# A one-core hybrid decoder layer: the load order of the DeltaNet stage, the planner's turns of small products, and the engine that forms the decayed queries

## The chip, the core and the metric

The kernel runs on one core of a Trainium2 chip. That core has five engines with instruction queues of their own: TensorE (PE in the profile, with its weight loads as PEld), VectorE (DVE), ScalarE (ACT), GpSimd (POOL) and SyncE (SP), which here does nothing but issue DMAs. The metric is the device time of one execution in microseconds. The kernel before was timed in three runs: 966.21, 965.89 and 964.76 us, median 965.89 us.

## The reference, cut to what matters

One layer is computed: 528 tokens (16 meta tokens and 512 of the input) of width 2048, normalised, projected by one wide matrix into the inputs of three mixers, whose outputs are joined and projected back. The change touches the first mixer, gated DeltaNet, with 6 heads of 128. Per chunk of tokens it needs the inverse of a unit lower triangular matrix, built from key products and decays:

```
a_mat = where(strict, einsum('bhncd,bhnsd->bhncs', kb, kc) * decay, 0)
u, w  = triangular_solve(eye + a_mat, [v * beta, kb * exp(g)])
qk    = where(causal, einsum('bhncd,bhnsd->bhncs', qc, kc) * decay, 0)
q_dec = qc * exp(g)
k_dec = kc * exp(g_last - g)
# per chunk, in order:
v_new = u - w @ s
o     = q_dec @ s + qk @ v_new
s     = s * g_last + k_dec^T @ v_new
```

The other two mixers are gated linear attention (GLA, 5 heads) and forgetting attention (5 heads); then come the output projection, the residual and a last normalisation.

## The kernel before, in words

All matrices are fp32. The wide products split their operands into two parts and use three matmuls with 512 (or, in a seven-product scheme, 264) moving columns; these read a weight tile of 128x128 each. The small products inside the mixers use plain fp32.

The work is written as generators (chains). A planner, `Weave` (L210 to L355), runs them against a table of costs (`cost`, L201) and emits one fixed program: every engine's instructions stand in the planned order, and the chip cannot change it. When an operand comes later than planned, the engine waits at that instruction and everything behind it on that engine waits too. A DMA is planned as one shared queue: bytes at 350 KB per microsecond, and then a fixed time to land (`DMAL`, L85, for loads; `STL` for stores to DRAM).

The planner distinguishes two kinds of TensorE work. An operation is "light" (L184) when it has under 64 moving columns, or fewer than 128 rows or columns of weights. In the DeltaNet stage these are the tiles `pm` (32x32), `pn` (64x64) and `pym` (16 rows), in GLA the tile `pss`. All else counts as heavy, the 128x128 products of the DeltaNet core (`pks`, `p1`, `po`) too. Lines L340 to L351 set the turns:

```
ran = t - self.since
if self.mode:
    other = ran + (sum(o.dur for o in c[3]) if c[3][0].light else 0.0) > LIGHT
else:
    other = ran >= HEAVY
...
    like = [x for x in self.chains if isinstance(x[3], list) and x[3][0].eng == "P"
            and x[3][0].light == kind and x[4] <= t + NEAR]
```

A turn of light work ends when it would pass `LIGHT`, if heavy work is ready within `NEAR`; when the best candidate is itself heavy, only what has already run is compared with `LIGHT`, and one more light list may be taken. A heavy turn ends after `HEAVY` (1.5), if light work is ready within `NEAR`. All of these are the planner's microseconds.

The stages in order of time are these. Up to 491 us the wide input projections run (`pz`, `pg`, `pbdz`, `px`). While they run, the score matrices of both DeltaNet head groups (`ans[0]`, `ans[1]`, three heads each) are made in `an_block` and stored to DRAM, and `inverse` (L695) inverts their 32x32 diagonal blocks on VectorE in a tile `ab`, stored to `sc2` at its end. Sixteen further projection blocks, the FILL list (`pbgq`, `pbfq`, `pbgz`, `pbfz`), are independent of all this. From 476 us on the planner puts them between the small products, and later takes the output projection's matmuls (`po` with 512 columns) for the same purpose.

The DeltaNet stage begins in `phase_b` (L1020). For each group g of three heads:

- `dn_rows(g)` (L1054) issues loads on SP: the score matrices `an`, keys `kT`, scaled values `vp`, queries `qT` and decayed keys `kd`. Group 1 waits until group 0 is through.
- `dn_group(g)` (L1077) loads the inverted blocks: `xc` and `xm` from `sc2`, and the meta rows `kdm`, `vpm`. Group 1 waits for `e_first`, which group 0 sets when its loads are out and its `levels` chain is started.
- `levels` and `level64` (L1099, L1139) combine 32x32 inverses to 64 and 128 with `pm` and `pn`; `state0` (L1163) makes the state after the meta tokens with `pym`.
- `core` (L1200) walks four blocks of 128 tokens. `pre` (L1182) prepares each block: it loads the decays `eg`, masks them on GpSimd into `at`, takes exponentials on ScalarE, multiplies `eg` by the queries (the decayed queries) on GpSimd, and forms the masked scores. `tail` (L1235) makes the block's output and normalises it.

## Time and profile before

| | us |
|---|---|
| median of three runs | 965.89 (964.76 to 966.21) |
| the profiled execution's own time | 967.15 |
| its span, first to last instruction | 964.6 |
| busy in the span: PE | 949.2 |
| PEld | 847.6 |
| DVE | 750.6 |
| ACT | 559.6 |
| POOL | 49.6 |

All instructions carry line L280, where the planner emits them, so the profile is read by tile names. Names are cut at digits: `an` stands for the score tiles, and also for the `eg` and `at` of `core`, which live in the same memory; `p` is `p1`; `po` with 128 columns belongs to `tail` and with 512 columns to the output projection. A fp32 matmul shows as two records. `SPq` is the queue on which SP issues DMAs. `PEclk` is the granted TensorE clock, 1.00 at full speed.

### The profile page before, as it was taken

To read this page: it belongs to the slowest core of one execution; us is meant where nothing else is said; L and a number is where in the kernel's file an instruction comes from. 1 tells how busy PE (TensorE), PEld (TensorE's weight loads), DVE (VectorE), ACT (ScalarE), POOL (GpSimd) and SP (SyncE) were. 2 spreads that over 40 slices of the span, in tenths; PEclk is the share of its full clock that TensorE was granted. 3 is DMA by queue.
4 is the path that set the end of the run, shared out by engine and by line. 5 is a ranking of instruction groups with operands and counts; after the bars stand their busy time and mean duration, and the time that the engine had idled before them with its cause. 6 is when DMAs were issued, how large, how long until landed. Compare 5 with 4: busy or idle time off the path is not lost.

```text
span 964.6 us, 18891 instructions
## 1 busy us (share of the span) xinstructions
PE 949.2 (98%) x7301; PEld 847.6 (88%) x7301; DVE 750.6 (78%) x1338; ACT 559.6 (58%) x1192; POOL 49.6 (5%) x94
## 2 busy tenths in 40 slices
PE   9999999999999999999999999999999999999996
PEld 7888999999999999999987897778787887888885
DVE  7986888888988787888983565886867976889874
ACT  7865566667656575754423675647555664335534
POOL 0000000000000000000010221101010100000000
PEclk9999999999999999999999899999999999999999
DMA  9933234436552535543188335424244246733105
GB/s 340 364 128 132 89 122 160 156 105 180 148 169 90 157 118 170 156 147 97 56 300 278 119 78 197 139 87 143 83 140 155 79 141 212 279 99 121 44 23 174
DMA packets 78893, 144.09 MB, mean 149 GB/s; under 512 B 14781, under 2 KB 35005, under 8 KB 78804
## 3 DMA queue, kind: packets, MB, share of 16 engines
q1 hardware_dynamic: 78516, 142.63, 45.0%
q8 instruction: 57, 0.93, 0.4%
q10 hardware_dynamic: 288, 0.27, 0.1%
q14 instruction: 32, 0.26, 0.1%
HBM read 119.26 MB, written 23.61 MB: 148 GB/s over the span
## 4 chain that ended last, share of the span: by engine, by line
PE 91%; DVE 3%; DMA 3%; ACT 2%; issue 1%; POOL 0%; DVEq 0%; SPq 0%; ACTq 0%; POOLq 0%
PE px L280 38%; PE po L280 11%; PE pz L280 6%; PE ps L280 6%; PE pbgz L280 5%; PE pbfz L280 5%; PE pbfq L280 4%; PE pbdz L280 2%; PE pfa L280 2%; PE pks L280 1%; PE pg L280 1%; PE pfw L280 1%; PE pss L280 1%; PE pbgq L280 1%; PE pgo L280 1%; DMA sc<-ab 1%
## 5 line engine op out<-in xcount | busy, mean ns | idle before, releaser
L280 DVE SCALAR_TENSOR_TENSOR lp<-a,hp 128x1024 fp32r<-128x1024 f32 x90 | 110.4, 1227 | 37.4 <-ACT hp L280 35.1
L280 ACT CAST hp<-a 128x1024 fp32r<-128x1024 f32 x90 | 94.4, 1049 | 71.8 <-PE px L280 44.0
L280 PE MATMUL px<-xh,hp 128*128 128x264 f32 x432 | 123.9, 287 | 0.0
L280 PE MATMUL px<-xh,lp 128*128 128x264 f32 x432 | 122.7, 284 | 0.0
L280 PE MATMUL px<-xl,hp 128*128 128x264 f32 x432 | 122.7, 284 | 0.0
L280 PE MATMUL px<-tah,hp 128*128 128x264 f32 x288 | 84.0, 292 | 0.0
L280 PE MATMUL px<-tbh,lp 128*128 128x264 f32 x288 | 82.3, 286 | 0.0
L280 PE MATMUL px<-tbh,hp 128*128 128x264 f32 x288 | 82.1, 285 | 0.0
L280 PE MATMUL px<-tbl,hp 128*128 128x264 f32 x288 | 82.0, 285 | 0.0
L280 PE MATMUL px<-tah,lp 128*128 128x264 f32 x288 | 81.9, 284 | 0.0
L280 PE MATMUL px<-tal,hp 128*128 128x264 f32 x288 | 81.8, 284 | 0.0
L280 PEld LDWEIGHTS px<-xh,hp 128*128 128x128 f32 x432 | 81.4, 188 | 0.0
L280 PEld LDWEIGHTS px<-xl,hp 128*128 128x128 f32 x432 | 81.2, 188 | 0.0
L280 PEld LDWEIGHTS px<-xh,lp 128*128 128x128 f32 x432 | 81.2, 188 | 0.0
L280 PE MATMUL po<-ho,oh 128*128 128x512 f32 x136 | 54.6, 402 | 0.0
L280 PEld LDWEIGHTS px<-tbh,hp 128*128 128x128 f32 x288 | 54.3, 189 | 0.1
L280 PEld LDWEIGHTS px<-tah,hp 128*128 128x128 f32 x288 | 54.2, 188 | 0.1
L280 ACT CAST hp<-s 128x1024 fp32r<-128x1024 f32 x36 | 37.8, 1050 | 28.4 <-PE px L280 20.9
L280 PEld LDWEIGHTS px<-tal,hp 128*128 128x128 f32 x288 | 54.3, 188 | 0.0
L280 PEld LDWEIGHTS px<-tbl,hp 128*128 128x128 f32 x288 | 54.2, 188 | 0.0
L280 PEld LDWEIGHTS px<-tah,lp 128*128 128x128 f32 x288 | 54.2, 188 | 0.0
L280 PEld LDWEIGHTS px<-tbh,lp 128*128 128x128 f32 x288 | 54.2, 188 | 0.0
(416 smaller groups left out, 2614.5 us busy)
## 6 DMA issues: line engine op xcount, KB each, us to landing
a<-in_w_in SPq DMA_DIRECT2D x72, 512.0 KB, 3.9
o<-in_w_out SPq DMA_DIRECT2D x20, 512.0 KB, 3.2
rgz<-in_w_in SPq DMA_DIRECT2D x10, 512.0 KB, 5.8
rfq<-in_w_in SPq DMA_DIRECT2D x10, 512.0 KB, 4.4
rfz<-in_w_in SPq DMA_DIRECT2D x10, 512.0 KB
xs<-in_xT SPq DMA_DIRECT2D x16, 264.0 KB, 5.5
fraw<-in_w_first SPq DMA_DIRECT2D x16, 256.0 KB
xt<-in_xtok SPq DMA_DIRECT2D x8, 512.0 KB
```

What stands on the lines that cost most here:

```text
L280: self.pin(op.call(*op.a, **op.kw))
```

## The change

The first part merges the two `dn_rows` chains into one with a new order: both groups' `an` first, then group 0's `kT` and `vp`, then a wait for `e_first`, and behind it group 0's `qT` and `kd` and all the rest of group 1. The second changes two constants of the planner: `LIGHT` from 3.0 to 2.2 and `NEAR` from 0.05 to 0.4. The third forms the decayed queries by `VT`, a scalar_tensor_tensor on VectorE, in place of a tensor_tensor on GpSimd.

```diff
-LIGHT, SLACK, DMAL, STL = 3.0, 0.25, 1.1, 2.5
-HEAVY, NEAR = 1.5, 0.05
+LIGHT, SLACK, DMAL, STL = 2.2, 0.25, 1.1, 2.5
+HEAVY, NEAR = 1.5, 0.4
...
-        for g in range(2):
-            W.go(dn_rows(g), LP + 0.1 * g, f"dnr{g}")
+        W.go(dn_rows(), LP, "dnrows")
...
-    def dn_rows(g):
-        s = gs[g]
-        if g:
-            yield e_rows[0]
-        s.an = yield Get(big_s, f"an{g}", (P, NN, P))
-        for b in range(NB):
-            yield e_an[g, b]
-        yield SP.dma_start(out=s.an, in_=ans[g])
-        e_anl[g].set()
-        s.kT = yield Get(big_s, f"kT{g}")
-        s.qT = yield Get(big_s, f"qT{g}")
-        for j in range(H):
-            yield from fetched(("dk", H * g + j), s.kT[:, j], Ev())
-        s.vp = yield Get(big_s, f"vp{g}", (P, NN, P))
-        yield SP.dma_start(out=s.vp, in_=vps[g])
-        for j in range(H):
-            yield from fetched(("dq", H * g + j), s.qT[:, j], Ev(), False)
-        s.kd = yield Get(keep_s, f"kd{g}")
-        yield SP.dma_start(out=s.kd, in_=kds[g])
-        e_rows[g].set()
+    def dn_rows():
+        for g in range(2):
+            gs[g].an = yield Get(big_s, f"an{g}", (P, NN, P))
+            for b in range(NB):
+                yield e_an[g, b]
+            yield SP.dma_start(out=gs[g].an, in_=ans[g])
+            e_anl[g].set()
+        for g in range(2):
+            s = gs[g]
+            s.kT = yield Get(big_s, f"kT{g}")
+            s.qT = yield Get(big_s, f"qT{g}")
+            if g:
+                yield e_first
+            for j in range(H):
+                yield from fetched(("dk", H * g + j), s.kT[:, j], Ev())
+            s.vp = yield Get(big_s, f"vp{g}", (P, NN, P))
+            yield SP.dma_start(out=s.vp, in_=vps[g])
+            if not g:
+                yield e_first
+            for j in range(H):
+                yield from fetched(("dq", H * g + j), s.qT[:, j], Ev(), False)
+            s.kd = yield Get(keep_s, f"kd{g}")
+            yield SP.dma_start(out=s.kd, in_=kds[g])
+            e_rows[g].set()
...
-        yield G.tensor_tensor(out=eg, in0=eg, in1=s.qT[:, :, ts], op=ALU.mult)
+        yield VT(out=eg, in0=eg, in1=s.qT[:, :, ts], op=ALU.mult)
```

## The prediction

> **What bounds the kernel now.** The page first, to see which engine sets the time:

> ```profile
> span 964.6 us, 18891 instructions
> PE 949.2 (98%) x7301; PEld 847.6 (88%) x7301; DVE 750.6 (78%) x1338; ACT 559.6 (58%) x1192; POOL 49.6 (5%) x94
> ```

> TensorE is busy for 949.2 of 964.6 us, and the change takes no matmul away. So time can come only from two places: moments in which TensorE stands, and moments in which it runs slowly. Its waits by tile come next (tile, releaser, total us, times, longest):

> ```profile
> PE pkd L280 <- DVE gst L280: 1.2, 2, 0.8
> PE pm L280 <- DVE uc L280: 1.0, 1, 1.0
> PE pss L280 <- issue: 0.9, 1, 0.9
> PE po L280 <- ACT f L280: 0.9, 1, 0.9
> ```

> Each is small. Two of them, `pm` and `po`, lie in the DeltaNet stage. For slow running I read the busy times by windows of 3.41 us there: first of everything, with the granted clock after the engines, then of the instructions that touch tile `pbgz` alone, the wide filler.

> ```profile
> 523.31:526.73 3.42, 3.22 (x151) 2.89 (x144) 1.85 (x6) 2.35 (x5) 0.00 (x0) 1.00 0.77 253
> 526.73:530.14 3.41, 3.41 (x38) 2.70 (x37) 0.92 (x5) 2.45 (x7) 0.00 (x0) 1.00 1.02 386
> 530.14:533.55 3.41, 3.41 (x34) 2.17 (x35) 0.00 (x0) 0.80 (x2) 0.00 (x0) 0.50 0.99 366
> 533.55:536.97 3.42, 3.42 (x120) 3.19 (x110) 1.52 (x3) 2.47 (x5) 1.75 (x4) 1.00 0.08 22
> 536.97:540.38 3.41, 3.41 (x19) 2.66 (x18) 2.21 (x7) 2.77 (x4) 0.00 (x0) 0.50 0.02 5
> ```

> ```profile
> 523.31:526.73 3.42, 1.20 (x5) 1.03 (x6) 0.00 (x0) 1.00 0.77 253
> 526.73:530.14 3.41, 0.46 (x2) 0.02 (x1) 0.00 (x0) 1.00 1.02 386
> 533.55:536.97 3.42, 0.00 (x0) 0.00 (x0) 0.00 (x0) 1.00 0.08 22
> ```

> The clock is 0.50 in exactly two windows, 530.14 to 533.55 and 536.97 to 540.38. Each follows a window that held almost nothing but small products: 0.46 and 0.00 us of wide matmuls. The window with 1.20 us of them was followed by full speed. PE was busy through the bad windows too (3.41 of 3.41), so standing still isn't the cause here; the kind of work is. What the half clock costs is read from the chain of waits, in order of time (start, length, what):

> ```profile
> 506.40 7.79 DMA sc<-ab
> 514.25 5.31 DMA xc<-sc
> 525.60 1.59 PE pbgz L280 x6
> 530.41 2.86 PE pbgz L280 x6
> 534.34 1.54 PE pn L280 x24
> 536.74 1.34 PE pks L280 x6
> 538.08 1.28 PE pbgz L280 x3
> 539.36 2.02 PE pn L280 x24
> 541.38 0.86 PE pks L280 x6
> ```

> The same pieces at both speeds: six `pbgz` 2.86 against 1.59 (+1.27), six `pks` 1.34 against 0.86 (+0.48), three `pbgz` 1.28 against half of 1.59 (+0.48), 24 `pn` 2.02 against 1.54 (+0.48). Together **2.7 us**; 3.4 is the most that two half-speed windows can cost.

> **The change, part by part.**

> *Shorter turns (`LIGHT` 3.0 to 2.2).* By the cost table of the code a `pn` or `pym` list counts 0.68, the first `pm` list 0.67, the second 1.34. The turn before 530.14 was `pym`, two `pn`, `pym`: 2.8 with the entry of 0.1, under 3.0. Under 2.2 it is cut after three lists, and the two other long turns of the stage after two or three. The longest turn then counts 2.15 or so where it counted 3.5, and a heavy turn of 1.5 stands behind it, two lists of three wide matmuls, 1.59 us on the chip. A window of 3.41 us then holds at least about 1 us of wide work, near the 1.20 that kept full speed and far from 0.46. I take both half-speed windows as gone: **-2.7**, with ends 0 and -3.4. Wide work has to be at hand for it: the chain shows `pbgz` before and after each of the long turns. More turns cost entries, by the timeline:

> ```profile
> 705.83 0.51 DVE L280 SCALAR_TENSOR_TENSOR qx<-gqT,gd 128x256 f32<-128x256 f32 x1
> 706.08 0.39 PE L280 MATMUL pbgz<-xl,hbgz 128*128 128x512 f32 x1
> 706.31 0.40 PE L280 MATMUL pbgz<-xh,lbgz 128*128 128x512 f32 x1
> 706.64 0.43 PE L280 MATMUL pss<-qx,kx 64*32 64x32 f32 x33
> ```

> Wide to wide is 0.23 us, wide to small 0.33: 0.1 for an entry. Three more turns are **+0.3**. GLA hardly changes: its lists of 64 products count 1.79, and two of them passed 3.0 already.

> *`NEAR` 0.05 to 0.4.* The planner may now place a small product up to 0.4 us before its operand. If the chip were as late as the plan, each of some 18 turns (6 in DeltaNet; in GLA four lists of `gla_levels` for each of three pairs) could wait 0.4 more, 7 us in all. But at 706.64 above, the operand `qx` was done at 706.34, 0.30 ahead, and this is the shortest lead among the GLA turns: the chip is earlier than the plan there. So 0.1 here and there, I take **+0.2**, ends 0 and +7. The transposes with 16 columns in the projection stage become candidates only after ScalarE operations that follow their operand, so `NEAR` moves none of them.

> *The loads.* The DMA issues from 490.4 to 506.4, up to the store `sc<-ab`, and from there to 519.6, when `xc` is in:

> ```profile
> DMA packets 1896, 5.65 MB, mean 353 GB/s; under 512 B 205, under 2 KB 205, under 8 KB 1895
> qT<-spdq SPq DMA_DIRECT2D x3, 256.0 KB
> kd<-kds SPq DMA_DIRECT2D x1, 768.0 KB
> ```

> ```profile
> rfq<-in_w_in SPq DMA_DIRECT2D x2, 512.0 KB
> an<-ans SPq DMA_DIRECT2D x1, 768.0 KB
> kT<-spdk SPq DMA_DIRECT2D x2, 264.0 KB
> ```

> Ahead of the store, `qT` and `kd` (1536 KB) leave and group 1's `an` (768 KB) enters: 768 KB less, 2.2 us at 353 GB/s. Between store and `xc`, `an` and two `kT` leave (1296 KB), 3.7 us. I expect the 13.1 us of the two transfers (7.79 + 5.31) to become about 8: a load of the size of `xc` takes 4.8 in the row below, and the store then the other 3.

> ```profile
> an<-gd SPq DMA_DIRECT2D x16, 192.0 KB, 4.8
> ```

> DeltaNet starts 5 us sooner, but TensorE had filler in nearly all of that time, so only the standing before `pm` counts:

> ```profile
> 518.84 0.40 PE L280 MATMUL pbgz<-xh,lbgz 128*128 128x512 f32 x1
> 520.22 0.95 PE L280 MATMUL pm<-uc,an 32*32 32x32 f32 x48 [0.99 <-DVE uc L280]
> ```

> 1.38 from start to start, less 0.23: 1.15. It arose since the chip's two transfers were later than planned behind a full queue; an emptier queue brings both nearer to the plan. **-1.15**, ends -1.15 and +5.9 (the case is a rival below). What is late next: the moved `qT`, `kd` and group 1's rows (4.6 MB, 13 us at 353 GB/s) aren't wanted before the core's products, the first of which is `pks` at 536.74; they are issued from about 512, so they are in by 526. On SP they stand behind both groups' `xc`, as group 1's rows stood behind group 0's. Nothing else is queued behind them but filler weights, of which a half block is always loaded ahead.

> *The decayed queries.* POOL's product is replaced by one on DVE. The groups by line in 546 to 580, and the busy times of 540 to 580:

> ```profile
> L280 POOL TENSOR_TENSOR an<-an,qT 128x384 f32<-128x384 f32 x8 | 8.0, 1001 | 17.7 <-DVE egl L280 16.0 <-PE po L280 1.5
> L280 DVE TENSOR_TENSOR an<-p,an 128x384 f32<-128x384 f32 x8 | 4.4, 552 | 0.8 <-PE p L280 0.8
> 540.00:560.00 20.00, 20.00 (x179) 18.92 (x179) 14.17 (x43) 13.99 (x49) 6.52 (x8) 0.99 0.34 93
> 560.00:580.00 20.00, 19.08 (x162) 18.24 (x161) 11.48 (x36) 14.87 (x66) 5.29 (x8) 1.00 0.37 87
> ```

> Eight instructions of 0.55 instead of 1.0: DVE +4.4, POOL -8.0. In that stretch PE stands once, 0.9 before `po`; all else is hidden by unbroken PE work, and DVE has 5.8 and 8.5 us free of 20. If that cover were gone, 0.55 per block would be bare, 4.4 at most. At the one bare place, the last block, DVE is the late engine, and 0.55 more would lengthen the wait to 1.4; POOL's shorter wait (1.0 to 0.55) gives up to 0.45. I take **0**, ends -0.9 and +4.4.

> **Sum** against the profiled execution's own 967.15: -2.7 + 0.3 + 0.2 - 1.15 + 0 = -3.35, so 963.8. That execution is 1.26 above the median of the runs shown, 965.89; taken off, the forecast is **962.5**.

> [...]

> **The rivals.**

> *The half clock stays.* The turns don't get short enough: when the best candidate is a heavy one, only what has run is compared with 2.2, and after 2.1 one more list may follow, 2.8 planned and some 3.1 us on the chip. A window could then hold 0.3 us of wide work, less than the 0.46 that was followed by 0.50. For it: the turn of 533.2 counted 3.5 under a limit of 3.0, by that very rule. Against it: the loads start DeltaNet elsewhere in the windows, and two windows of that kind must come again. 962.5 + 2.7 = **965.2**.

> *The order moves further than the data (slower).* The plan takes the removed bytes off at its own rate, up to 5.9 us, and sets `pm` that much sooner; if the chip's store and load get only half of it, TensorE stands for 1.15 + 3 at `pm`, more than a window's length, and one half-speed window follows (1.7 more). From a lag of 3.4 us on it eats up the whole gain. For it: the chip was later than the plan at this place already. Against it: the store waited behind bytes that really go. 962.5 + 1.15 + 3 + 1.7 = **968.4**.

> *More than forecast.* The new order also halves the other waits shown (`pkd` 1.2, `pss` 0.9, `po` 0.9: 3.0). Nothing in the change aims at `pkd`; 962.5 - 1.5 = **961.0**.

> **Chances.** The forecast 0.50, the half clock stays 0.24, the order outruns the data 0.15, more than forecast 0.11. A run of this kernel can tell about 0.2% (1.93 us) from no change, so faster means under 963.96. The forecast's own range is 960.5 to 964.3; with more than forecast, less a little beyond the edge, faster gets 0.58. Half clock makes no difference that counts: same 0.27. Slower 0.15. The range 959.6 to 967.8 takes in the first, second and last case, and leaves out most of the slower one.

> **What would show it.** Right: no window at 0.50 between the first `pm` and `pks`; every small turn under about 2.6 us, with `pbgz` or `pbfq` between; `sc<-ab` and `xc<-sc` at some 3 and 5 us; the wait of `pm` on `uc` gone from the list. Wrong: clock 0.50 again in the stage (first rival); `pm` waiting for over 2 us on `xc` (second); a new wait of `po` or `pks` for a product of DVE; waits of `pss` for `qx` in GLA, which would be `NEAR`.

## The result, and the profile after

The changed kernel takes **981.01 us** (median of four runs, 975.38 to 982.84) against 965.76 us for the kernel before in the same comparison. The ratio is 1.015, with a 95% interval of 1.0107 to 1.0192: slower, far outside the range of the prediction. All ratios here leave out executions that took over 1.5% longer than the fastest of the same kernel, while the medians and ranges keep them. The profiled execution after took 982.84 us, 15.7 us more than the profiled execution before.

The page of the changed kernel first: span, busy times, and the granted clock in 40 slices.

```profile
span 981.1 us, 18903 instructions
PE 962.2 (98%) x7301; PEld 857.2 (87%) x7301; DVE 754.0 (77%) x1346; ACT 558.3 (57%) x1192; POOL 41.7 (4%) x86
PEclk9999999999999999999997599999999999999999
```

TensorE runs as many matmuls as before, is busy 13.0 us longer, and its clock dips in the slices from about 515 to 565 us, the DeltaNet stage. Its waits there (tile, releaser, total us, times, longest):

```profile
PE pm L280 <- issue: 3.1, 1, 3.1
PE pm L280 <- DVE uc L280: 2.1, 2, 1.1
```

The wait of `pm` on `uc`, 1.0 before, is now 2.1. New is a stand of 3.1 us in `pm` for which the profile names no operand at all ("issue"). In both traces the granted clock changes on the borders of windows of 3.41 us (530.14, 533.55, 536.97 and 540.38 before; 529.36 and 560.08 here). Such windows, then of some of them the filler `pbgz` alone:

```profile
525.95:529.36 3.41, 0.27 (x28) 0.15 (x14) 2.50 (x6) 1.23 (x3) 0.00 (x0) 1.00 0.94 341
529.36:532.77 3.41, 3.41 (x17) 2.33 (x17) 2.03 (x8) 2.52 (x5) 0.41 (x1) 0.50 1.01 409
...
556.67:560.08 3.41, 3.41 (x19) 3.41 (x17) 1.38 (x4) 1.54 (x4) 0.00 (x0) 0.50 0.00 0
560.08:563.49 3.41, 3.41 (x26) 2.88 (x25) 3.07 (x8) 2.61 (x4) 0.00 (x0) 1.00 0.01 2
```

```profile
529.36:532.77 3.41, 2.00 (x5) 1.62 (x6) 0.00 (x0) 0.50 1.01 409
532.77:536.19 3.42, 0.93 (x3) 0.20 (x1) 0.00 (x0) 0.50 1.06 414
536.19:539.60 3.41, 1.95 (x5) 1.56 (x6) 0.00 (x0) 0.50 0.96 243
```

In the window of the stand TensorE was busy 0.27 of 3.41 us. From then on it is busy all the time, but at half speed for **nine windows in a row**, 529.4 to 560.1. Before, it was at half speed for two. (The last 2 to 5 us of the span, too, run at half speed in every profile here; they are left out in what follows.) Last, the chain of waits of the changed kernel (start, length, what):

```profile
507.77 6.59 DMA sc<-ab
...
516.51 3.00 DMA xc<-sc
519.51 0.02 issue
519.53 0.59 DVE uc L280
520.12 0.04 issue
520.17 0.95 PE pm L280 x48
521.11 1.58 PE pbgz L280 x6
522.70 0.95 PE pm L280 x66
523.65 1.59 PE pbgz L280 x6
525.24 0.90 PE pm L280 x63
526.14 3.14 issue
529.28 0.28 PE pm L280 x4
529.56 1.27 PE pym L280 x6
530.84 2.86 PE pbgz L280 x6
533.70 4.03 PE pn L280 x36
537.73 2.86 PE pbgz L280 x6
540.58 4.03 PE pn L280 x36
```

The turns are as short as planned: three lists of `pn` and then six `pbgz`, over and over. What the plan didn't hold is the stand at 526.14, in the middle of a list whose operands were all there, and half clock for everything behind it.

**The account of the 16.5 us of span.** Half speed lasts 30.7 us where it lasted 6.8, and half of the difference, 11.9 us, is the most that it can cost. The two standing rows of `pm` come to 5.2 where they came to 1.2 (a row of 0.2 for "issue" was there before), +4.0. And 1.4 us were lost ahead of the stage, where the matmuls stand in the same order in both kernels: the first load of scores is issued at 490.43 before and at 491.80 after. That is 17.3, a little more than 16.5, since the first term is an upper end.

```profile
490.43 0.39 SPq L280 DMA_DIRECT2D an<-ans  x1
```

```profile
491.80 0.39 SPq L280 DMA_DIRECT2D an<-ans  x1
```

**Where the stand comes from.** The profile counts the packets that bring instructions by a kind of their own. In the changed kernel they are:

```profile
q1 hardware_dynamic: 78516, 142.63, 44.5%
q8 instruction: 57, 0.93, 0.4%
```

57 packets of 16 KB on q8 stand beside 7301 matmul records and as many weight loads: some 256 instructions each, half of them matmuls. The fp32 `pm` products are two matmul records each, so a block is some 64 of them. No view shows where a block ends, its edge. So I took the stand at 526, 3.3 us from record to record, for an edge (record 4052), and counted matmul records from there. The stands inside lists of `pss` that the profile puts down to "issue", in the runs below, come at records 5062, 5189 and 5949: 8, 9 and 15 blocks further on, if a block holds 126.4 matmul records (why not 128 isn't shown). The same holds for all 14 profiles of this document: beyond the first 30 us, TensorE stands 25 times for over 0.3 us on "issue", and each of these stands is within 5 records of such an edge. A wait for instructions would look like this: the block before the stand was used up in 2.76 us, 11 ns an instruction, the next packet (526.83 to 528.15) started only 3.6 us after the edge at 523.19, when TensorE stood already, and TensorE resumed 1.1 us after the packet's end.

So two theories stood against each other. The **fetch theory**: the new order puts both groups' `pm` lists back to back, and beside them a wave of loads (4.6 MB, issued from 519.6 on); TensorE uses up blocks of instructions faster than they arrive and stands, and half clock follows (0.50 behind the window at 525.95, which was busy for 0.27 of 3.41 us). The **data theory**, the prediction's slower rival: the order asks for `xc` or the moved rows sooner than they come. Third, that one of the two small edits did it.

### The profile page after: what moved, and what is told of

Same layout as the page of the kernel before. It is cut to its first block, busy times and chain, and to the rows that moved or that the text cites. A ratio compares the mean times of both kernels' runs of the same rounds, so it can differ in the third digit from the quotient of the medians.

```text
span 981.1 us, 18903 instructions
## 1 busy us (share of the span) xinstructions
PE 962.2 (98%) x7301; PEld 857.2 (87%) x7301; DVE 754.0 (77%) x1346; ACT 558.3 (57%) x1192; POOL 41.7 (4%) x86
## 4 chain that ended last, share of the span: by engine, by line
PE 90%; DVE 4%; ACT 2%; DMA 2%; issue 1%; SPq 0%; POOL 0%; DVEq 0%; POOLq 0%; ACTq 0%
PE px L280 37%; PE po L280 10%; PE pz L280 6%; PE ps L280 6%; PE pbgz L280 5%; PE pbfz L280 5%; PE pbfq L280 4%; PE pbdz L280 2%; PE pks L280 2%; PE pg L280 1%; PE pfw L280 1%; PE pfa L280 1%; PE pgo L280 1%; PE pbgq L280 1%; PE pn L280 1%; PE pss L280 1%
## 5 line engine op out<-in xcount | busy, mean ns | idle before, releaser
L280 DVE SCALAR_TENSOR_TENSOR lp<-a,hp 128x1024 fp32r<-128x1024 f32 x90 | 110.7, 1230 | 36.9 <-ACT hp L280 36.4
L280 ACT CAST hp<-a 128x1024 fp32r<-128x1024 f32 x90 | 94.4, 1049 | 71.0 <-PE px L280 43.9
L280 PE MATMUL px<-xh,hp 128*128 128x264 f32 x432 | 123.9, 287 | 0.0
L280 PE MATMUL px<-xh,lp 128*128 128x264 f32 x432 | 122.7, 284 | 0.0
L280 PE MATMUL px<-xl,hp 128*128 128x264 f32 x432 | 122.7, 284 | 0.0
L280 PE MATMUL px<-tah,hp 128*128 128x264 f32 x288 | 84.0, 292 | 0.0
L280 PE MATMUL px<-tbh,lp 128*128 128x264 f32 x288 | 82.3, 286 | 0.0
L280 PE MATMUL px<-tbh,hp 128*128 128x264 f32 x288 | 82.1, 285 | 0.0
L280 PE MATMUL px<-tbl,hp 128*128 128x264 f32 x288 | 82.0, 285 | 0.0
L280 PE MATMUL px<-tah,lp 128*128 128x264 f32 x288 | 81.9, 284 | 0.0
L280 PE MATMUL px<-tal,hp 128*128 128x264 f32 x288 | 81.8, 284 | 0.0
L280 PEld LDWEIGHTS px<-xh,hp 128*128 128x128 f32 x432 | 81.4, 188 | 0.0
L280 PEld LDWEIGHTS px<-xl,hp 128*128 128x128 f32 x432 | 81.2, 188 | 0.0
L280 PEld LDWEIGHTS px<-xh,lp 128*128 128x128 f32 x432 | 81.2, 188 | 0.0
L280 PE MATMUL po<-ho,oh 128*128 128x512 f32 x136 | 54.4, 400 | 0.0
L280 PEld LDWEIGHTS px<-tbh,hp 128*128 128x128 f32 x288 | 54.3, 189 | 0.1
L280 PEld LDWEIGHTS px<-tah,hp 128*128 128x128 f32 x288 | 54.3, 188 | 0.1
L280 PEld LDWEIGHTS px<-tal,hp 128*128 128x128 f32 x288 | 54.3, 188 | 0.0
L280 ACT CAST hp<-s 128x1024 fp32r<-128x1024 f32 x36 | 37.8, 1050 | 28.9 <-PE px L280 21.4
L280 PEld LDWEIGHTS px<-tah,lp 128*128 128x128 f32 x288 | 54.2, 188 | 0.0
L280 PEld LDWEIGHTS px<-tbl,hp 128*128 128x128 f32 x288 | 54.2, 188 | 0.0
L280 PEld LDWEIGHTS px<-tbh,lp 128*128 128x128 f32 x288 | 54.2, 188 | 0.0
## 6 DMA issues: line engine op xcount, KB each, us to landing
a<-in_w_in SPq DMA_DIRECT2D x72, 512.0 KB, 3.9
o<-in_w_out SPq DMA_DIRECT2D x20, 512.0 KB, 3.1
rgz<-in_w_in SPq DMA_DIRECT2D x10, 512.0 KB, 6.6
rfq<-in_w_in SPq DMA_DIRECT2D x10, 512.0 KB, 3.6
rfz<-in_w_in SPq DMA_DIRECT2D x10, 512.0 KB
xs<-in_xT SPq DMA_DIRECT2D x16, 264.0 KB, 5.5
fraw<-in_w_first SPq DMA_DIRECT2D x16, 256.0 KB
xt<-in_xtok SPq DMA_DIRECT2D x8, 512.0 KB
```

The lines of the kernel that those rows point to most:

```text
L280: self.pin(op.call(*op.a, **op.kw))
```

## The experiments

Each compares with runs of the kernel before on the same chip. All compute the whole layer.

**The three edits, one at a time.** First the load order alone, with the old constants and the product on GpSimd:

```diff
-LIGHT, SLACK, DMAL, STL = 2.2, 0.25, 1.1, 2.5
-HEAVY, NEAR = 1.5, 0.4
+LIGHT, SLACK, DMAL, STL = 3.0, 0.25, 1.1, 2.5
+HEAVY, NEAR = 1.5, 0.05
...
-        yield VT(out=eg, in0=eg, in1=s.qT[:, :, ts], op=ALU.mult)
+        yield G.tensor_tensor(out=eg, in0=eg, in1=s.qT[:, :, ts], op=ALU.mult)
```

> The new load order alone, planner's constants and GpSimd product as before. Theory A (the burst of late loads, 4.6 MB behind e_first, falls on the small products, makes TensorE stand about 3 us in the middle of a pm list and so halves the clock): a stand of 2 to 4 us at pm or pn, 15 to 30 us at half clock, 972 to 982 us. Theory B (the short turns keep the clock at half once it has dropped: no window holds enough wide work): at most the two or three half-speed windows of before, 963 to 969 us. Theory C (both parts are needed): as B here and no loss with the turns alone either.

Measured: 979.17 us (972.36 to 981.72), ratio 1.0129 (1.0079 to 1.0178). Its waits:

```profile
PE pss L280 <- issue: 5.2, 3, 3.3
...
PE pm L280 <- issue: 1.5, 1, 1.5
PE pm L280 <- DVE uc L280: 1.1, 1, 1.1
```

The order alone brings nearly the whole loss. Half clock comes in five single windows here, four of them in the stage. The stand in `pm` is 1.5, less than the 2 to 4 expected; the larger stands of this execution are in `pss`. The wait on `uc` is 1.1, as before, so it explains none of the loss. What is new are the stands for which the profile names no operand, and the half-speed windows.

Next the two constants alone, in the kernel before:

```diff
-LIGHT, SLACK, DMAL, STL = 3.0, 0.25, 1.1, 2.5
-HEAVY, NEAR = 1.5, 0.05
+LIGHT, SLACK, DMAL, STL = 2.2, 0.25, 1.1, 2.5
+HEAVY, NEAR = 1.5, 0.4
```

> LIGHT 2.2 and NEAR 0.4 alone, loads and GpSimd product as before. Theory A: no long stand, since the burst is not there; 962 to 967 us. Theory B: a drop of the clock in the stage as before, and then over 15 us at half clock, 972 to 980 us. Theory C: 962 to 967 us.

Measured: 965.73 us (963.4 to 978.21, ten runs), ratio 1.001 (0.998 to 1.004): no difference. The profiled execution has no half-speed window between 20 us and its last 10 us, so in this execution the shorter turns have taken both windows away, and the time doesn't show it.

Then the product on VectorE alone, in the kernel before:

```diff
-        yield G.tensor_tensor(out=eg, in0=eg, in1=s.qT[:, :, ts], op=ALU.mult)
+        yield VT(out=eg, in0=eg, in1=s.qT[:, :, ts], op=ALU.mult)
```

> The decayed queries on VectorE alone. All three theories: no difference that can be measured, 964 to 967.5 us, the half-speed windows of before unchanged. If the product on VectorE were what costs, 968 us or more with new waits of po for a VectorE product.

Measured: 969.72 us (963.3 to 976.35, ten runs), ratio 1.003 (0.9996 to 1.0064): not told from no change.

```profile
PE pss L280 <- issue: 4.3, 3, 3.3
...
PE po L280 <- DVE an L280: 0.8, 1, 0.8
```

The product itself shows up as 0.8 at the one bare place, where the kernel before waits 0.9 on ScalarE's `f`. The 970.26 us of the profiled execution have another source: a stand of 3.3 us in a `pss` list, on an edge of a block, and 6.8 us at half speed behind it. Its runs spread over 13 us.

**The two halves of the new order.** Both score matrices first, with no wait for `e_first`, old constants, old product (against the changed kernel, beside the constants and the product shown above):

```diff
-            if g:
-                yield e_first
...
-            if not g:
-                yield e_first
```

> Of the new load order only its first half: both groups' score matrices first, then all rows without the wait for the inverse's loads; planner's constants and GpSimd product as before. Theory F: the wave is through before the small products, fetches start within 1.5 us of entering a block; close lists may still give a stand of up to 1 us; 964 to 970 us. If bringing the groups' lists together were enough by itself: 972 us or more, with the stand of 1.5 us or more that the whole new order alone showed.

Measured: 966.22 us (963.84 to 970.35, ten runs), ratio 1.0004 (0.9981 to 1.0028). The other half, the rows behind `e_first` with group 1's score matrix among them:

```diff
     def dn_rows():
         for g in range(2):
+            s = gs[g]
             gs[g].an = yield Get(big_s, f"an{g}", (P, NN, P))
             for b in range(NB):
                 yield e_an[g, b]
             yield SP.dma_start(out=gs[g].an, in_=ans[g])
             e_anl[g].set()
-        for g in range(2):
-            s = gs[g]
```

> The second half of the new load order alone: group 0's queries and decayed keys and all of group 1's rows, its score matrix too, wait for the signal of group 0 before they are issued; group 1's score matrix is no longer issued ahead. Old turn constants, GpSimd product. Fetch theory: it needs both, the two groups' pm lists close together and a wave of loads beside them. Here group 1's score matrix comes in the wave itself, so group 1's lists lie some 5 us behind group 0's, a block of instructions lasts over 5 us, and the stand in pm is under 1.5 us: 964 to 971. If the wave alone does it: a stand of 2.5 us or more in a pm list and half clock behind it, 972 to 982. Data theory (operands that come late for group 1): waits of pm on uc of 2 us or more, 968 to 972.

Measured: 970.47 us (968.75 to 975.53, ten runs), ratio 1.0039 (1.0012 to 1.0065).

```profile
PE pss L280 <- issue: 1.6, 2, 0.9
PE pm L280 <- DMA an<-ans: 1.2, 1, 1.2
```

No list of `pm` stands for "issue" here; one waits 1.2 for its scores, which come in the wave. One half costs nothing, the other 0.4%, together 1.3%. That doesn't show that it takes closeness and wave at once, since neither run has the two groups' lists close together. With the scores first and no wait, `xc` again stands behind the rows, the first `pm` starts at 520.4 (520.2 in the kernel before), and the second block of instructions lasts 8.0 us. With the rows behind `e_first`, it lasts 12.6.

**Scores first with the two constants**, the change without the wave and without the product (the run above with the constants 2.2 and 0.4):

> Scores first alone (both groups' score matrices ahead, no wait for the signal) together with the two turn constants, the product on GpSimd: the change without the wave of loads. Fetch theory: the loads are spread as before, no stand over 1.5 us in pm or pss; the short turns keep the clock full in the stage: 963.5 to 967, about as fast as the kernel before. If closeness of the two groups' pm lists alone starves TensorE: a stand over 2 us in pm and 972 or more.

Measured: 966.64 us (964.34 to 974.0, ten runs), ratio 1.0021 (0.9994 to 1.0047). Not told from the kernel before, and so no gain. The profiled execution is one of its long ones, 974.0:

```profile
PE pss L280 <- issue: 5.3, 2, 4.1
PE pm L280 <- DVE uc L280: 2.0, 1, 2.0
```

No `pm` list stands for its instructions here, but these lists are also less dense: the blocks last 4.8 and 6.3 us. A `pss` list in GLA does stand, for 4.1 us in this execution. I hadn't expected that.

**Taking the cause apart.** In the changed kernel, the wave held back until both groups have their first inverse:

```diff
-                yield e_first
+                yield (e_u[0], e_u[1])
```

(at both places.)

> The changed kernel with the second wave of loads (group 0's qT and kd, group 1's kT, vp, qT, kd) held until both groups' inverses are planned, behind all pm and pn. Theory F (TensorE stands in the middle of a pm list because its next 16 KB of instructions come late; the fetch starts 3.6 us after TensorE enters the block when the wave fills the queues, some 1 us when they are quiet; and the block of small products is crossed in under 3 us): the fetch in the pm stretch starts within 1.5 us, the stand falls from 3.3 to 1 us or less, 964 to 972 us. Theory D (the stand is a wait for data that the profile does not name): operands and order are the same, the stand stays at 2.5 us or more, 975 us or more.

Measured: 977.86 us (975.6 to 980.27), ratio 1.0109 (1.0066 to 1.0152).

```profile
PE pss L280 <- issue: 3.2, 2, 2.3
...
PE ps L280 <- ACT wh L280: 1.7, 2, 1.2
PE ps L280 <- DVE wl L280: 1.4, 3, 1.0
```

The stand in `pm` is gone, as the fetch theory has it: with the DMA engines nearly idle, the packet came 0.7 us after the edge at 521.8. The blocks also lasted longer, 5.4 and 4.6 us. But the time isn't gained, and the expected 964 to 972 was missed: by tile, 4.5 us more than in the kernel before go to `ps` and 2.2 to `po` of the output. The last `pss` ends at 803.7, at 762.2 in the kernel before, while the last filler product ends at 775.5 (776.5 before). The output stage then waits on ScalarE and VectorE for its operands; that the one brings the other was not tested. Keeping the groups apart instead, group 1's `levels` held until group 0 has its inverse:

```diff
+        if g:
+            yield e_u[0]
         W.go(levels(g), -0.2, f"levels{g}", LSL)
```

> The changed kernel with group 1's levels started only when group 0's inverse is planned, so that the two groups' pm and pn lists do not stand close together; loads as in the changed kernel. Theory F: the block of instructions is crossed in 5 us or more, so even a late fetch is hidden; no stand over 0.6 us within a pm list, under 11 us at half clock, 963 to 970 us. Theory D: a stand of 1 us or more stays, or moves to the list's new place.

Measured: 976.3 us (975.06 to 979.28), ratio 1.0105 (1.0068 to 1.0142). Again no stand in `pm`, one half-speed window in the stage, and 4.6 us more in `ps`; 963 to 970 was expected. In both runs the stand is gone, but neither prices it, since each also moves the work behind it.

Heavier turns in the changed kernel, so that the small lists stand further apart:

```diff
-HEAVY, NEAR = 1.5, 0.4
+HEAVY, NEAR = 3.4, 0.4
```

> The changed kernel with HEAVY 3.4 in place of 1.5: wide turns of some five lists, 3.5 us, at least a window long at full speed. Theory A: the stand of about 3 us at pm stays, and the clock stays at half while the loads last, 974 to 982 us. Theory B: the clock recovers within one or two windows of each drop, under 14 us at half clock in all, 966 to 972 us, the rest of the loss being the stands at pm. Theory C: as B.

Measured: 972.45 us (971.59 to 973.06), ratio 1.0069 (1.0054 to 1.0084), half clock in single windows only, and 0.9 us of stand on the same edge. About half of the loss is gone. The same idea in the kernel before, smaller light turns and larger heavy ones:

```diff
-LIGHT, SLACK, DMAL, STL = 3.0, 0.25, 1.1, 2.5
-HEAVY, NEAR = 1.5, 0.05
+LIGHT, SLACK, DMAL, STL = 1.4, 0.25, 1.1, 2.5
+HEAVY, NEAR = 2.6, 0.4
```

> The kernel before with turns paced to the fetch: LIGHT 1.4, HEAVY 2.6, NEAR 0.4, so that about one list of small products is followed by four wide lists, 2.8 us. Theory F: no stand over 0.6 us within a list of pm or pss, no long-tailed executions, 962 to 965 us in every one. Theory D, or if the stands depend on data: stands within pss as in the kernel before (1.1 us) and executions of 968 us and more as now.

Measured: 999.48 us (994.83 to 1003.42), ratio 1.0334 (1.0271 to 1.0396).

```profile
PE po L280 <- DVE acc L280: 4.0, 1, 4.0
PE ps L280 <- ACT wh L280: 3.9, 2, 2.7
```

Both expectations failed: a `pss` list still stood for 0.9 us on an edge, and the time was some 35 us above the 962 to 965 expected. By tile, the output stage pays: 13.5 us more in `po` and 12.1 in `ps`. The last filler product ends at 764.2, the last `pss` at 834.3.

**Moving the edges.** These two runs decide about the stand. If blocks of instructions are cut by position alone, products ahead of a list move the edges in it, whatever its operands. At the start of TensorE's program stand nine warm-up matmuls whose results nobody reads. Two of them were replaced by 34 tiny ones, which puts every later instruction 32 products, half a block, further on. The order of all other products is that of the changed kernel, but for three small ones of the projection stage (`pr`), which stand a few places earlier.

```diff
-        yield [PE.matmul(pw[:, :P], ones, ones, start=True, stop=True) for _ in range(9)]
+        yield [PE.matmul(pw[:, :P], ones, ones, start=True, stop=True) for _ in range(7)]
+        yield [PE.matmul(pw[:32, :32], ones[:, :32], ones[:, :32], start=True, stop=True) for _ in range(34)]
```

> The changed kernel with two of the nine warm-up matmuls replaced by 34 tiny ones (32x32), so that everything behind them, in an unchanged order, stands 32 products (64 records) further on in TensorE's instruction stream. Fetch theory: the stand of 3.3 us comes from a 16 KB block of instructions that isn't there yet, so it moves with the block's edge, 64 records forward in the program: in the changed kernel it lay after the 90th of 96 records of a pm list, here it must lie after about the 26th of the same list, 2.5 to 3.5 us long, and end 1.1 to 1.5 us after the end of a 16 KB instruction packet. Time 975 to 984. Data theory: the stand belongs to an operand or a transfer that is late for a certain instruction; it stays after the 90th record. A chance stall of the chip: it is gone or elsewhere, and the time is 968 or less.

Measured: **969.35 us** (967.42 to 984.01, ten runs), ratio 1.0038 (1.0006 to 1.0071). Two of the ten are long, 977.58 and 984.01, at a clock of 0.985 and 0.980; they left no trace. The profiled execution was the shortest. The control moves everything by a whole block, so that the edges fall where the changed kernel has them:

```diff
-        yield [PE.matmul(pw[:, :P], ones, ones, start=True, stop=True) for _ in range(9)]
+        yield [PE.matmul(pw[:, :P], ones, ones, start=True, stop=True) for _ in range(2)]
+        yield [PE.matmul(pw[:32, :32], ones[:, :32], ones[:, :32], start=True, stop=True) for _ in range(71)]
```

> The changed kernel with seven of the nine warm-up matmuls replaced by 71 tiny ones: the order of all other products is that of the run shifted by 32, but they stand 64 products, 256 instructions, further on than in the changed kernel, one whole block. If the run shifted by half a block was fast since the edges of the blocks fell elsewhere in the pm lists, the edges are here back where the changed kernel has them: a stand of 2.5 to 4 us after the 90th of 96 records of a pm list, half clock for 10 us or more behind it, 975 to 984. If it was fast for what the shorter warm-up or a planned start did, or by chance: no such stand, 967 to 971.

Measured: **980.55 us** (972.82 to 991.01, four runs), ratio 1.014 (1.0051 to 1.0229). Without the longest execution of each, the medians are 974.5 here and 969.2 with half a block, and the two intervals just overlap, so the times alone don't decide. The traces do. The record behind the stand in the timelines of the changed kernel, of the half block and of the whole block (the stand is in brackets):

```profile
529.28 0.18 PE L280 MATMUL pm<-xc,m 32*32 32x32 f32 x1 [3.14 <-issue]
```

```profile
525.38 0.18 PE L280 MATMUL pm<-xc,m 32*32 32x32 f32 x1 [0.33 <-issue]
```

```profile
530.15 0.18 PE L280 MATMUL pm<-xc,m 32*32 32x32 f32 x1 [3.11 <-issue]
```

And the edges counted through the three traces and that of the kernel before:

```
kernel        edges crossed at (us)       us between    packet after    stand on the
                                                        second edge     last edge
changed       518.72  523.19  525.95      4.5   2.8     526.83-528.15   3.3, after record 90 of 96
whole block   519.53  524.08  526.84      4.6   2.8     527.76-528.74   3.3, after record 90 of 96
half block    511.38  522.08  524.87     10.7   2.8     522.91-523.93   0.5, after record 26 of 96
before        520.62  524.13  533.55      3.5   9.4     528.80-529.73   none
```

The stand sits on the edge of a block, whatever the instruction there: shifted by 64 records it is 64 records earlier in the same list, shifted by a whole block it is back behind the same record. That is the fetch theory; a late operand would have held up the same instruction each time. It isn't the longer warm-up either, which is longest in the run that has the stand back. One number of the expectation failed: I had put the moved stand at 2.5 to 3.5 us, and it was 0.3 (0.5 from record to record), with a time below the 975 to 984 expected. The packet for the edge at 524.87 had come 0.8 us after the edge ahead of it, not 3.6 or 3.7. I took the 10.7 us of slow work before that edge for the reason, but it isn't shown: with the heavier turns a block of 8.2 us stood there, and the packet came 3.4 us after.

The changed kernel has a bad place for its edges. In its own trace the shortest time for two blocks in the stage is 7.2 us (10.5 in the kernel before), and its edges fall on just those, though pairs that begin later contain the stand itself. In the half-block trace the same products have their shortest pair, 6.5 us, eight records further on.

And the loads need not be what is new. In the kernel before, too, the DMA engines were 90% busy behind the second edge, and the packet came 4.7 us after it, later than in the changed kernel. Nothing stood, since the block lasted 9.4 us. In GLA, in the run with the order alone, a packet came some 3.4 us after an edge (639.2 to 642.6) with the DMA engines at 0.00. What the changed kernel has and the kernel before lacks is a block that is used up in 2.8 us from edge to edge; what the wave adds isn't separated.

With half a block, the profiled execution, the shortest of ten, shows no half-speed window in the stage at all, and the same pieces at full speed (two lines of its chain):

```profile
528.42 2.24 PE pn L280 x36
530.66 1.58 PE pbgz L280 x6
```

That is 2.24 against 4.03 and 1.58 against 2.86. Of the 969.35 us, the longer warm-up itself takes 1.4 (the first wide matmul starts at 6.59, at 5.19 in the changed kernel), so the changed order with its edges there is at about 968. In the control the warm-up takes 3.0 (8.18), which leaves 977.6, or 971.5 without its longest execution. Its profiled execution, 974.54, has three half-speed windows in the stage, not nine. No run here showed a version that beats the kernel before.

## Why the prediction was wrong, point by point

**The failed step** lies in "The loads": TensorE "had filler in nearly all of that time, so only the standing before `pm` counts", and behind the moved rows "Nothing else is queued" but filler weights. I took a list as running through once its operands are there, and had no term for TensorE waiting for its own instructions. That was put at nothing. In its place the runs showed a stand of 3.3 us inside a `pm` list, on the edge of a block that was used up in 2.8 us, and half clock behind it. Half a block of shift makes the difference from the changed kernel some 12 us: the ratios 1.015 and 1.0038 are 10.8 us apart, and the warm-up takes another 1.4. How much of this is the packet held up by the moved loads, and how much the closer lists alone, stays open.

**The slower rival** named the right place and sign and the wrong mechanism. `pm` did stand for over 3 us, and half speed followed, but on instructions, not on `xc`; it gave one half-speed window and 968.4, and there were nine. The rival's last term, 1.7 for a half-speed window behind a stand longer than a window, had no row beside it in the prediction; the traces have two such places. In the changed kernel it is the stand itself: 0.27 of 3.41 us busy at 525.95, then 0.50 for 30.7 us. In the kernel before it is the end of the span, left out elsewhere: 0.41 of 3.41 us busy from 956.81 to 960.22, then 0.50. For half speed that lasts over several busy windows I had no term.

**The two transfers.** 7.79 + 5.31 were to become 3 + 5. They became 6.59 and, for group 1's `xc`, 3.00; group 0's first `pm` starts at 518.09, after a stand of 0.96. Allowing for the 1.37 us that this execution was late at 491, that is 3.5 us sooner than 520.22, not 5. The store gained only 1.2 from 768 KB less ahead of it. The wait of `pm` was to vanish (-1.15); there are two of them now, one for each group, 2.1 in all.

**The shorter turns.** The mechanism held as far as seen: turns are short, and neither the run with the constants alone nor the half-block run has a half-speed window in the stage. (The run with scores first and the constants has one at 522.0, behind the wait of 2.0 on `uc`.) The size, -2.7, didn't carry over to the median. I took it from one profiled execution with a clock of 0.994; the kernel before has a median clock of 0.995 to 0.997 in the 65 runs beside these experiments, so most of its executions probably have fewer of these windows, and there was less to gain.

**What keeps half speed going** may be in the prediction's rows, read further. Six `pbgz` at half speed take 2.86. Before, they fell nearly whole into the window 530.14, and in the control run into 531.09; both were followed by full speed:

```profile
530.14:533.55 3.41, 2.93 (x6) 1.82 (x6) 0.00 (x0) 0.50 0.99 366
```

```profile
531.09:534.50 3.41, 2.78 (x6) 1.69 (x6) 0.00 (x0) 0.51 1.03 410
534.50:537.91 3.41, 1.54 (x6) 1.05 (x6) 0.00 (x0) 0.99 1.02 379
```

In the changed kernel a turn of six and three lists of `pn` take 6.9 us at half speed, about two windows, and the six lie across the border of two windows each time: 2.00 and 0.93, 1.95 and 0.98, 1.89 and 1.04, none followed by full speed. The last half-speed window, 556.67, held only 0.07 of `pbgz`, but 128x128 products throughout (`pks` and `p`). So the rows fit a rule by the share of wide work in a window, if the 128x128 products count as wide. The phase of the turns against the windows would then decide how long half speed lasts, which would fit the spread of the control run (972.8 to 991.0). Neither was tested alone.

**What half speed starts behind.** In the prediction's rows both halvings followed a window that was busy throughout (3.41 of 3.41 us at 526.73, 3.42 of 3.42 at 533.55). In the changed kernel the window at 525.95, busy for only 0.27 of 3.41 us while `pm` stood, is followed by half speed, and in the half-block run, with the stand at 0.3 us, no half-speed window shows in the stage. Both kinds of halving occur.

**`NEAR` and the product on VectorE** were put at +0.2 and 0. Alone they can't be told from nothing; the waits on `qx` in the run with the constants are 0.8 in all, and the bare place of the product cost 0.8 where 0.9 stood before.

## What to carry to other kernels

In this kernel small matmuls outran the supply of their own instructions: a block of 256 was used up in 2.8 us, while the next packet started 3.6 us after the block's first edge. When a schedule packs many of them close together, count the instructions per microsecond over two blocks (7.2 us for two in the changed kernel, which stood, and 10.5 in the kernel before, which didn't in that stage), and look for "issue" stands inside a list whose operands are there. If one turns up, shift the stream by half a block with harmless instructions before explaining it by data: the stand moves or it doesn't (here it moved from behind record 90 of a list to behind record 26). And a change that brings dense lists closer together needs a term for this in its forecast, even where every operand comes in time.
